# Up products of an MLP with both token parts in one 512-column matmul, and norm factors moved behind the down product

## The chip, the cores and the metric

The kernel runs on one NeuronCore of a Trainium2 chip. The metric is the device time of one execution in microseconds (us), the median of three runs.

## The reference, cut to what matters

The network has two parts. The first block has two layers (DEPTH = 2) over T = 256 tokens of width D = 1024: attention and convolution branches ("mix"), then an MLP of hidden width 4096. The second block has another attention and a product-key expert layer ("peer"). The change is in the MLP of the first block:

```python
def rmsnorm(x, g):
    y = xf * lax.rsqrt(jnp.mean(xf * xf, axis=-1, keepdims=True) + EPS)
    return (y * g.astype(jnp.float32)).astype(x.dtype)
...
        u = rmsnorm(x, norm_mlp[l])
        x = x + jnp.square(jax.nn.relu(u @ w_mlp_up[l])) @ w_mlp_down[l]
```

The norm's factor is one positive number for each token, so it can be left out of `u` and applied later: to the up product's result once, or, squared, to the down product's result.

## The kernel before, in words

**Split products.** Every fp32 operand of a large matmul is a sum of two parts, hi and lo, and each product is three matmuls: hi with hi, hi with lo, lo with hi. A `Stream` loads weights in blocks of 128x1024 or so (`raw`, by SyncE's DMA queue); ACT copies the hi part (`whi`, L92), DVE subtracts for the lo part (`wlo`, L93). There are six buffers for `whi` and `wlo`, and the splits run six blocks ahead: L92 of block j+6 writes the buffer that block j's matmuls have just read, and so it waits for the last matmul of block j that reads `whi`.

**The up stage.** The hidden width is made in 32 chunks of 128. One chunk is one weight block and eight pieces of the width D (KC = 8). `wtype` issues for each piece the three matmuls of `mm3` (L121 hi with hi, L122 hi with lo, L123 lo with hi), each 256 columns (the tokens): 24 matmuls for a chunk. The first four chunks (`split_first`) use four PSUM buffers `pf`. The other 28 go in 14 pairs: a pair shares one PSUM buffer `pw` [128, 2, 256] of the pool `psw`, which has two buffers. When both chunks of the pair are done, DVE takes relu times the norm factors (L673, `rl` from `pw` and `rows`, 512 columns), ACT squares into `hhi` (L675), DVE squares `rl` in place (L676) and subtracts for `hlo` (L677).

**The norm factors.** `factor_rows` turns the two columns of factors into a tile `rows` with a factor for each token along the free axis: two transposes on PE (L276) and a copy on ACT (L277), once a layer, behind the first four chunks.

**The down stage.** `ttype` multiplies `hhi` and `hlo` with the down weights into four accumulators (`acc`, matmuls L357 to L359) and `add` (L196) adds each 128x512 result to `x` on DVE. `norm_twice_cols` does the same for the last layer, with the next norms.

**What sets the order.** The framework's scheduler lays down each engine's instructions in one fixed order when the program is built. Each engine then works through its list in order; an instruction that waits for a semaphore holds up all that stand behind it on that engine. What one buffer costs when it is still in use is such a wait.

**In the peer part** the same products for the query and expert weights are already made with 8 matmuls of 512 columns (L926: `whi` with hi and lo of the tokens side by side) and 8 of 256 (L928: `wlo` with hi) for a block; ACT then copies one half of the PSUM buffer (L931) and DVE adds the other half (L932).

Of the kernel before, what the change touches and what calls it, by code (L numbers as in the profile page):

```python
# [18 lines left out]
P = 128  # L19
T = 256  # L20
NT = 2
D = 1024
KC = D // P
# [13 lines left out]
PK = 16  # L37
# [79 lines left out]


def mm3(nc, out, a, b, first, last):
# [73 lines left out]

def add(k, x, t, h, acc):
    s = x[:, t, h * 512:(h + 1) * 512]
    k.nc.vector.tensor_tensor(out=s, in0=acc[t][h], in1=s, op=ALU.add)  # L196

# [45 lines left out]

def scaled_cols(k, stream, x, norm, first=False):

    nc = k.nc
    u = [k.acts.tile([P, KC, T], F32R, name=n, tag=n) for n in ("uhi", "ulo")]
    gB = k.work.tile([P, D], F32, name="gB", tag="gB", bufs=2)  # L250
    nc.sync.dma_start(out=gB, in_=norm.to_broadcast([P, D]))
    xg = [k.work.tile([P, D], F32, name="xg", tag="xn", bufs=2) for _ in range(NT)]
    done = []

    def each(acc, t, h):
        c = slice(h * 512, (h + 1) * 512)
        if acc is not None:
            add(k, x, t, h, acc)
# [20 lines left out]

def norm_twice_cols(k, stream, pool, x, acc, fB, gB, sB, hi, lo):  # L280

# [33 lines left out]
    with k.tc.manual_schedule(engines={nc.vector.engine}):  # L315
        add(k, x, 0, 0, acc)
        times(0, 0, nc.vector)
        scaled(0, 0, nc.gpsimd)
        add(k, x, 0, 1, acc)
# [4 lines left out]
        add(k, x, 1, 0, acc)  # L324
        times(1, 0, nc.gpsimd)
        scaled(1, 0, nc.gpsimd)
        hi_part(0, 0)
        add(k, x, 1, 1, acc)
        hi_part(0, 1)
# [79 lines left out]


def split_first(k, stream, u, n):


    pss = [k.psa.tile([P, T], F32, name="pf", tag="acc") for _ in range(n)]
    ws = [stream.next(i) for i in range(n)]
    for part in (range(0, 4), range(4, KC)):
        for ps, w in zip(pss, ws):
            end = wtype(k, w, 0, u, KC, ps, part)
    return pss, end
# [109 lines left out]
def layer(k, l, stream, x, u, rs):  # L529
# [3 lines left out]
    with k.tc.tile_pool(name="att", bufs=1, reuse_waits="tile") as att:  # L533
# [107 lines left out]
        ttype(k, stream, (mhi, mlo), 8, 1, 512, 2, tail=TAIL_MIX, swap=True, each=each)  # L641
    rows = k.work.tile([P, T], F32, name="rows", tag="rows", bufs=1)
    rs = factors()
    with k.tc.tile_pool(name="mlp", bufs=1, reuse_waits="tile") as mlp:
# [15 lines left out]
        first, end = split_first(k, stream, u, FIRST)  # L660
        with k.tc.issue_after(end):
            factor_rows(k, rs, rows)
        for j in range(0, HID // P, 2):
            r = mlp.tile([P, 2, T], F32, name="rl", tag="rl", bufs=3)
            if first:
                for i in range(2):
                    nc.vector.scalar_tensor_tensor(out=r[:, i, :], in0=first.pop(0), scalar=0.0, in1=rows,
                                                   op0=ALU.max, op1=ALU.mult)
            else:
                ps = k.psw.tile([P, 2, T], F32, name="pw", tag="w")  # L670
                for i in range(2):
# [12 lines left out]
        if l < DEPTH - 1:  # L684
            u, each, factors = scaled_cols(k, stream, x, k.a["norm_mix"][l + 1:l + 2, :], True)
# [5 lines left out]
        u = [k.acts.tile([P, KC, T], F32R, name=n, tag=n) for n in ("uhi", "ulo")]  # L691
        norm_twice_cols(k, stream, mlp, x, acc, *last[0], *u)
        return u, None

# [210 lines left out]

def peer(k, x, pool, hp, stream, u, both):

# [3 lines left out]
    with ExitStack() as es:  # L911
# [8 lines left out]
        def up(e2, done, gl):  # L920

            w = stream.next()
            ps = k.psa.tile([P, 2, T], F32, name="pw", tag="acc")
            for c in range(KC):
                o = slice(c * P, (c + 1) * P)
                nc.tensor.matmul(ps.rearrange("p i t -> p (i t)"), w[0][:, o], both[:, c].rearrange("p i t -> p (i t)"),  # L926
                                 start=c == 0, stop=False)
                end = nc.tensor.matmul(ps[:, 0, :], w[1][:, o], u[0][:, c, :], start=False, stop=c == KC - 1).ins  # L928

            def total(out, part):  # L930
                nc.scalar.activation(out, ps[:, 1, part], AF.Copy)  # L931
                nc.vector.tensor_tensor(out=out, in0=ps[:, 0, part], in1=out, op=ALU.add)  # L932
                nc.scalar.activation(out, out, AF.Gelu_apprx_tanh)
# [23 lines left out]
        with k.tc.tile_pool(name="tk", bufs=1, reuse_waits="tile") as tk:  # L957
# [26 lines left out]
            def select():  # L984
                for h in range(H):
# [16 lines left out]
                    if h % 2 == 0:  # L1002
                        vs = tk.tile([P, 2, NT, PK], F32, name="vs", tag="vs", bufs=2)
                    vi = tk.tile([P, NT, PK], U32, name="vi", tag="vi", bufs=2)
                    for t in range(NT):
# [216 lines left out]
def body(tc, a):  # L1222
# [3 lines left out]
    with ExitStack() as es:  # L1226
# [21 lines left out]
        with ExitStack() as ph:  # L1248
# [22 lines left out]
            hp = es.enter_context(tc.tile_pool(name="hp", bufs=1, side="right", reuse_waits="tile"))  # L1271
            both = hp.tile([P, KC, 2, T], F32R, name="h2", tag="h2")
            u = [both[:, :, 0, :], both[:, :, 1, :]]
# [4 lines left out]
        peer(k, x, pool, hp, stream, u, both)  # L1278

# [117 lines left out]
```

## Time and profile before

| | us |
|---|---|
| median of 3 runs | 1693.84 |
| the runs | 1691.16 to 1696.8 |
| the profiled execution, its time | 1690.12 |
| its span, first to last instruction | 1688.3 |

In the rows below, times are us from the start of the span, unless they are marked ns. An engine's "busy" is the time in which one of its instructions ran. "[0.87 <-DVE wlo L93]" behind an instruction says that its engine sat idle for 0.87 us before it, until line 93 on DVE had written `wlo`. A matmul's end is modelled and successive matmuls overlap; what one costs is the distance from its start to the next start.

### The profile page before, as it was taken

Reading aid. Unit: us, or ns where it says so; the run is one execution under the profiler, and the core shown is the slowest. Engines: PE = TensorE matmul, PEld = TensorE weight load, DVE = VectorE, ACT = ScalarE, POOL = GpSimd, SP = SyncE. Lnnn points to the kernel's source line nnn. Section 1 sums busy time; section 2 is a strip of 40 time slices with the busy share of each in tenths; the row PEclk is TensorE's granted clock in tenths of the full one; section 3 lists DMA queues with packets and bytes.
Section 4 is the critical chain, followed back from the end, with each engine's and each line's share of the span. In section 5 each row is a group of like instructions: output and inputs, shape, how many; then the busy total and the mean of one; then the engine's idle time right before and its main releaser. Section 6 shows DMA issues by size and latency. Waiting matters only on the chain.

```text
span 1688.3 us, 27147 instructions
## 1 busy us (share of the span) xinstructions
PE 1653.2 (98%) x10082; PEld 1468.1 (87%) x10082; DVE 1296.1 (77%) x2257; ACT 906.3 (54%) x1575; POOL 299.1 (18%) x227
## 2 busy tenths in 40 slices
PE   8999999999999999999999999999999999999997
PEld 7899899888999999878878889888888787888886
DVE  6867788767867778866768999998999876555555
ACT  6554545336554544344555665667777544444443
POOL 1000000000000000025400586777810000000000
PEclk9999999999999999999999999999999999999999
DMA  8566578976456667967226678777755887666664
GB/s 315 180 198 218 192 241 293 366 258 200 139 152 185 214 199 257 360 203 241 88 80 195 179 178 204 176 177 168 159 153 164 263 281 224 190 191 193 190 193 129
DMA packets 115715, 345.58 MB, mean 205 GB/s; under 512 B 29856, under 2 KB 31104, under 8 KB 114688
## 3 DMA queue, kind: packets, MB, share of 16 engines
q1 hardware_dynamic: 95104, 336.23, 61.7%
q0 software_dynamic: 20480, 7.63, 4.2%
q8 instruction: 79, 1.29, 0.3%
q14 instruction: 52, 0.43, 0.1%
HBM read 342.66 MB, written 11.64 MB: 210 GB/s over the span
## 4 chain that ended last, share of the span: by engine, by line
PE 79%; DVE 11%; DMA 4%; ACT 2%; issue 2%; POOL 1%; SPq 0%; POOLq 0%; DVEq 0%; ACTq 0%
PE acc L358 12%; PE acc L357 12%; PE acc L359 12%; PE pw L123 9%; PE pw L121 9%; PE pw L122 9%; PE pw L926 8%; PE pw L928 4%; DVE wlo L93 4%; DMA gt<-gscr 3%; PE pst L1095 1%; PE po L477 1%; ACT whi L92 1%; DVE big L932 1%; DVE big L1097 1%
## 5 line engine op out<-in xcount | busy, mean ns | idle before, releaser
L93 DVE TENSOR_TENSOR wlo<-raw,whi 128x1024 fp32r<-128x1024 f32 (+1 forms) x549 | 669.0, 1221 | 211.9 <-ACT whi L92 209.2
L92 ACT ACTIVATE whi<-raw 128x1024 fp32r<-128x1024 f32 (+1 forms) x549 | 572.9, 1047 | 481.9 <-PE acc L359 210.2
L926 PE MATMUL pw<-h,whi 128*128 128x512 f32 x1024 | 362.9, 398 | 0.0
L928 PE MATMUL pw<-h,wlo 128*128 128x256 f32 x1024 | 285.6, 279 | 0.0
L121 PE MATMUL pw<-uhi,whi 128*128 128x256 f32 x1000 | 285.1, 285 | 0.0
L122 PE MATMUL pw<-ulo,whi 128*128 128x256 f32 x1000 | 284.2, 284 | 0.0
L123 PE MATMUL pw<-uhi,wlo 128*128 128x256 f32 x1000 | 284.2, 284 | 0.0
L946 POOL DMA_INDIRECT gscr<-gate,place x128 | 221.5, 1730 | 130.2 <-DVE first L1049 67.2
L926 PEld LDWEIGHTS pw<-h,whi 128*128 128x128 f32 x1024 | 192.3, 188 | 43.0
L358 PE MATMUL acc<-wlo,ah 128*128 128x512 f32 x512 | 201.9, 394 | 0.9 <-DVE wlo L93 0.9
L357 PE MATMUL acc<-whi,ah 128*128 128x512 f32 x512 | 201.0, 393 | 1.7 <-DVE big L932 1.7
L359 PE MATMUL acc<-whi,al 128*128 128x512 f32 x512 | 198.7, 388 | 0.0
L122 PEld LDWEIGHTS pw<-ulo,whi 128*128 128x128 f32 x1000 | 192.4, 192 | 1.3 <-issue 1.3
L121 PEld LDWEIGHTS pw<-uhi,whi 128*128 128x128 f32 x1000 | 192.5, 192 | 0.9 <-issue 0.7
L928 PEld LDWEIGHTS pw<-h,wlo 128*128 128x128 f32 x1024 | 192.9, 188 | 0.2 <-DVE wlo L93 0.2
L123 PEld LDWEIGHTS pw<-uhi,wlo 128*128 128x128 f32 x1000 | 192.4, 192 | 0.7 <-issue 0.7
L357 PEld LDWEIGHTS acc<-whi,ah 128*128 128x128 f32 x512 | 96.1, 188 | 25.1 <-issue 2.8
L359 PEld LDWEIGHTS acc<-whi,al 128*128 128x128 f32 x512 | 96.1, 188 | 21.8 <-DVE al L128 0.4
L358 PEld LDWEIGHTS acc<-wlo,ah 128*128 128x128 f32 x512 | 96.3, 188 | 20.7 <-DVE wlo L93 1.7
L357 PE MATMUL acc<-whi,hhi 128*128 128x512 f32 x256 | 99.9, 390 | 0.0
L358 PE MATMUL acc<-wlo,hhi 128*128 128x512 f32 x256 | 99.8, 390 | 0.0
L359 PE MATMUL acc<-whi,hlo 128*128 128x512 f32 x256 | 99.6, 389 | 0.0
(265 smaller groups left out, 2524.3 us busy)
## 6 DMA issues: line engine op xcount, KB each, us to landing
raw<-in_w_layers_dram SPq DMA_DIRECT2D x240, 512.0 KB
raw<-in_u_dram SPq DMA_DIRECT2D x128, 512.0 KB
raw<-in_v_dram SPq DMA_DIRECT2D x128, 512.0 KB
aw<-in_w_ada_dram SPq DMA_DIRECT2D x48, 512.0 KB
gscr<-in_zeros_dram SPq DMA_DIRECT2D x16, 512.0 KB
raw<-in_w_query_dram SPq DMA_DIRECT2D x16, 512.0 KB
gt<-gscr SPq DMA_DIRECT2D x32, 256.0 KB
raw<-in_w_qkb_dram SPq DMA_DIRECT2D x8, 512.0 KB
```

The costliest lines, as they stand in the source:

```text
L92: self.nc.scalar.activation(hi[:, :w], r[:, :w], AF.Copy)
L93: self.last_split = self.nc.vector.tensor_sub(lo[:, :w], r[:, :w], hi[:, :w]).ins
L121: nc.tensor.matmul(out, a[0], b[0], start=first, stop=False)
L122: nc.tensor.matmul(out, a[0], b[1], start=False, stop=False)
L123: return nc.tensor.matmul(out, a[1], b[0], start=False, stop=last).ins
L357: nc.tensor.matmul(acc, a[0], w[0][:, o:o + cols], start=first, stop=False)
L358: nc.tensor.matmul(acc, a[0], w[1][:, o:o + cols], start=False, stop=False)
L359: return nc.tensor.matmul(acc, a[1], w[0][:, o:o + cols], start=False, stop=last).ins
L477: nc.tensor.matmul(po[:, h, :], pT[:, i, :], v[:, c, vcol(h):vcol(h) + DH], start=(c == 0), stop=(c == nchunk - 1))
L926: nc.tensor.matmul(ps.rearrange("p i t -> p (i t)"), w[0][:, o], both[:, c].rearrange("p i t -> p (i t)"), start=c == 0, stop=False)
L928: end = nc.tensor.matmul(ps[:, 0, :], w[1][:, o], u[0][:, c, :], start=False, stop=c == KC - 1).ins
L946: ins = nc.gpsimd.indirect_dma_start(out=k.gscr, out_offset=bass.IndirectOffsetOnAxis(ap=place[:, h, j:j + 1], axis=0), in_=gate[:, h, j:j ...
```

## The change

The two parts of `u` become one tile with hi and lo side by side (`parts`), and the MLP's up product uses the form of the peer part: `wtype_both` issues 8 matmuls of 512 columns and 8 of 256 for a chunk. Its result takes a whole `psw` buffer for one chunk, since the products with `u` hi and `u` lo lie in separate halves, and `halves` brings them together: a copy on ACT (L450) and an add on DVE (L451), 128x256 each, for each of the 64 chunks. Then DVE makes relu(r) times r (L712), ACT copies the hi part (L713) and DVE subtracts (L714), once for a pair. `factor_rows` goes from the MLP; its factors are squared (`squared`, two DVE instructions of 128x1 a layer) and `add` multiplies the down result with them while it adds (four instructions in each layer, 128x512 as before, with one more operand). `vi`, a small tile of the peer part, has one buffer where it had two.

```diff
+def wtype_both(k, w, u, nk, out, part=None):
+    for c in part or range(nk):
+        o = slice(c * P, (c + 1) * P)
+        k.nc.tensor.matmul(out.rearrange("p i t -> p (i t)"), w[0][:, o], u.both[:, c].rearrange("p i t -> p (i t)"),
+                           start=c == 0, stop=False)
+        end = k.nc.tensor.matmul(out[:, 0, :], w[1][:, o], u[0][:, c, :], start=False, stop=c == nk - 1).ins
+    return end
+
+def halves(k, out, ps):
+    k.nc.scalar.activation(out, ps[:, 1, :], AF.Copy)
+    return k.nc.vector.tensor_tensor(out=out, in0=ps[:, 0, :], in1=out, op=ALU.add).ins
...
-def add(k, x, t, h, acc):
+def add(k, x, t, h, acc, factors=None):
     s = x[:, t, h * 512:(h + 1) * 512]
-    k.nc.vector.tensor_tensor(out=s, in0=acc[t][h], in1=s, op=ALU.add)
+    if factors is None:
+        k.nc.vector.tensor_tensor(out=s, in0=acc[t][h], in1=s, op=ALU.add)
+    else:
+        k.nc.vector.scalar_tensor_tensor(out=s, in0=acc[t][h], scalar=factors[t], in1=s, op0=ALU.mult, op1=ALU.add)
...
-        with k.tc.issue_after(end):
-            factor_rows(k, rs, rows)
         for j in range(0, HID // P, 2):
             r = mlp.tile([P, 2, T], F32, name="rl", tag="rl", bufs=3)
-            if first:
-                for i in range(2):
-                    nc.vector.scalar_tensor_tensor(out=r[:, i, :], in0=first.pop(0), scalar=0.0, in1=rows,
-                                                   op0=ALU.max, op1=ALU.mult)
-            else:
-                ps = k.psw.tile([P, 2, T], F32, name="pw", tag="w")
-                for i in range(2):
-                    wtype(k, stream.next(), 0, u, KC, ps[:, i, :])
-                nc.vector.scalar_tensor_tensor(out=r, in0=ps, scalar=0.0,
-                                               in1=rows[:, None, :].to_broadcast([P, 2, T]), op0=ALU.max, op1=ALU.mult)
-            nc.scalar.activation(hhi[:, j:j + 2, :], r, AF.Square)
-            nc.vector.tensor_tensor(out=r, in0=r, in1=r, op=ALU.mult)
+            for i in range(2):
+                if first:
+                    ps = first.pop(0)
+                else:
+                    ps = k.psw.tile([P, 2, T], F32, name="pw", tag="w")
+                    wtype_both(k, stream.next(), u, KC, ps)
+                halves(k, r[:, i, :], ps)
+            nc.vector.scalar_tensor_tensor(out=r, in0=r, scalar=0.0, in1=r, op0=ALU.max, op1=ALU.mult)
+            nc.scalar.activation(hhi[:, j:j + 2, :], r, AF.Copy)
             up = nc.vector.tensor_sub(hlo[:, j:j + 2, :], r, hhi[:, j:j + 2, :]).ins
```

**DVE in the middle of layer 0's up stage, before:** two periods of a pair.

```order
L673 SCALAR_TENSOR_TENSOR rl<-pw,rows 128x512
L93 TENSOR_TENSOR wlo<-raw,whi 128x1024
L676 TENSOR_TENSOR rl<-rl 128x512
L677 TENSOR_TENSOR hlo<-rl,hhi 128x512
L93 TENSOR_TENSOR wlo<-raw,whi 128x1024
L673 SCALAR_TENSOR_TENSOR rl<-pw,rows 128x512
L93 TENSOR_TENSOR wlo<-raw,whi 128x1024
L676 TENSOR_TENSOR rl<-rl 128x512
```

**The same place of the change,** two periods (`pw` is the PSUM buffer of one chunk; the chunk whose L451 stands behind L714 is the even one of its pair, the next L451 is the odd one's):

```order
L93 TENSOR_TENSOR wlo<-raw,whi 128x1024
L714 TENSOR_TENSOR hlo<-rl,hhi 128x512
L451 TENSOR_TENSOR rl<-pw,rl 128x256
L93 TENSOR_TENSOR wlo<-raw,whi 128x1024
L451 TENSOR_TENSOR rl<-pw,rl 128x256
L712 SCALAR_TENSOR_TENSOR rl<-rl 128x512
L93 TENSOR_TENSOR wlo<-raw,whi 128x1024
L714 TENSOR_TENSOR hlo<-rl,hhi 128x512
L451 TENSOR_TENSOR rl<-pw,rl 128x256
L93 TENSOR_TENSOR wlo<-raw,whi 128x1024
L451 TENSOR_TENSOR rl<-pw,rl 128x256
```

Where one L673 for a pair stood between two weight splits, each chunk now has its own add. The even chunk's add stands third, behind the split (L93) of the block six further on and behind the last step (L714) of the pair before.

**ACT at that place, before and in the change:**

```order
L675 ACTIVATE hhi<-rl 128x512
L92 ACTIVATE whi<-raw 128x1024 x2
L675 ACTIVATE hhi<-rl 128x512
L92 ACTIVATE whi<-raw 128x1024 x2
L675 ACTIVATE hhi<-rl 128x512
L92 ACTIVATE whi<-raw 128x1024 x2
```

```order
L713 ACTIVATE hhi<-rl 128x512
L450 ACTIVATE rl<-pw 128x256
L92 ACTIVATE whi<-raw 128x1024
L450 ACTIVATE rl<-pw 128x256
L92 ACTIVATE whi<-raw 128x1024
L713 ACTIVATE hhi<-rl 128x512
```

The two copies L450 stand behind the weight splits L92, the even one behind L713 of the pair before as well. The first `L442` of a chunk carries a wait for the L451 of the chunk two before it, whose PSUM buffer it takes.

**PE near the end of layer 0's up stage in the change** (`acc` with `whi` and `hhi` is the down product):

```order
L442 MATMUL pw<-u,whi 128x512
L444 MATMUL pw<-u,wlo 128x256
L442 MATMUL pw<-u,whi 128x512
L444 MATMUL pw<-u,wlo 128x256
L383 MATMUL acc<-whi,hhi 128x512
L384 MATMUL acc<-wlo,hhi 128x512
L385 MATMUL acc<-whi,hlo 128x512
L383 MATMUL acc<-whi,hhi 128x512
L442 MATMUL pw<-u,whi 128x512
```

Four matmuls of the down product now stand in front of the first chunk of the last pair, and three in front of that of the pair before; so it is in both layers. In the kernel before no down product stands between the up products. Elsewhere in the program the order of PE, DVE, ACT and POOL is the same but for buffer numbers; in SyncE's queue some loads of the up stage changed places.

## Rows read from the trace of the kernel before

**Rows 1.** The page: busy time and share of the span; then the chain's engines.

```profile
PE 1653.2 (98%) x10082; PEld 1468.1 (87%) x10082; DVE 1296.1 (77%) x2257; ACT 906.3 (54%) x1575; POOL 299.1 (18%) x227
...
PE 79%; DVE 11%; DMA 4%; ACT 2%; issue 2%; POOL 1%; SPq 0%; POOLq 0%; DVEq 0%; ACTq 0%
```

**Rows 2.** Stretches: length, busy and instructions of each engine, clock, DMA; layer 0's up stage.

```profile
211.70:292.40 80.70, 80.70 (x675) 80.70 (x674) 68.87 (x85) 40.14 (x46) 1.02 (x2) 1.00 0.79 265
```

**Rows 3.** Groups by shape, same stage: count | busy, mean ns | idle before, releaser.

```profile
L121 PE MATMUL pw<-uhi,whi 128*128 128x256 f32 x224 | 63.5, 283 | 0.0
...
L93 DVE TENSOR_TENSOR wlo<-raw,whi 128x1024 fp32r<-128x1024 f32 x29 | 35.4, 1222 | 6.0 <-ACT whi L92 6.0
L92 ACT ACTIVATE whi<-raw 128x1024 fp32r<-128x1024 f32 x28 | 29.7, 1061 | 35.5 <-PE pw L122 21.6 <-issue 11.7 <-ACT hhi L675 1.2
```

**Rows 4.** Timeline, one pair's end in layer 0 (start, duration, engine, line).

```profile
240.58 0.28 PE L121 MATMUL pw<-uhi,whi 128*128 128x256 f32 x1
...
240.71 1.06 ACT L92 ACTIVATE whi<-raw 128x1024 fp32r<-128x1024 f32 x1 [1.82 <-PE pw L122]
240.78 0.69 DVE L673 SCALAR_TENSOR_TENSOR rl<-pw,rows 128x512 f32<-128x512 f32 x1 [0.63 <-PE pw L123]
...
241.81 1.22 DVE L93 TENSOR_TENSOR wlo<-raw,whi 128x1024 fp32r<-128x1024 f32 x1 [0.33 <-ACT whi L92]
...
242.95 0.68 DVE L676 TENSOR_TENSOR rl<-rl 128x512 f32<-128x512 f32 x1
...
243.67 0.69 DVE L677 TENSOR_TENSOR hlo<-rl,hhi 128x512 fp32r<-128x512 f32 x1
```

**Rows 5.** Timeline, peer part with its 512- and 256-column matmuls.

```profile
899.80 0.40 PE L926 MATMUL pw<-h,whi 128*128 128x512 f32 x1
...
902.40 0.41 DVE L932 TENSOR_TENSOR big<-pw,big 128x256 f32<-128x256 f32 x1
...
903.17 0.37 ACT L931 ACTIVATE big<-pw 128x256 f32<-128x256 f32 x1
...
905.00 0.39 PE L926 MATMUL pw<-h,whi 128*128 128x512 f32 x1
```

**Rows 6.** Timeline, PE between first chunks and the rest, layer 0.

```profile
211.46 0.28 PE L123 MATMUL pf<-uhi,wlo 128*128 128x256 f32 x1
...
211.58 0.38 PE L276 MATMUL pr<-ident,pw 128*128 128x128 f32 x2
...
211.72 0.36 PE L121 MATMUL pw<-uhi,whi 128*128 128x256 f32 x1
...
211.92 0.28 PE L122 MATMUL pw<-ulo,whi 128*128 128x256 f32 x1
```

**Rows 7.** Timeline, a PE wait for DVE in the value stage.

```profile
1394.88 1.22 DVE L93 TENSOR_TENSOR wlo<-raw,whi 128x1024 fp32r<-128x1024 f32 x1
...
1396.15 0.51 PE L358 MATMUL acc<-wlo,ah 128*128 128x512 f32 x1 [0.87 <-DVE wlo L93]
...
1396.49 0.40 PE L359 MATMUL acc<-whi,al 128*128 128x512 f32 x1
...
1396.73 0.40 PE L357 MATMUL acc<-whi,ah 128*128 128x512 f32 x1
```

**Rows 8.** Timeline, DVE, two instructions of 512 columns in a row.

```profile
197.25 0.69 DVE L260 TENSOR_TENSOR xg<-x,gB 128x512 f32<-128x512 f32 x1
...
197.86 0.68 DVE L182 TENSOR_TENSOR ulo<-pst,uhi 128x512 fp32r<-128x512 f32 x1
```

**Rows 9.** Stretches, columns as in rows 2: the first four chunks, layer 0.

```profile
199.20:211.70 12.50, 12.50 (x105) 12.22 (x104) 9.33 (x14) 9.71 (x17) 1.68 (x3) 1.00 0.44 137
```

**Rows 10.** Stretches, columns as in rows 2: start of the second block, peer part.

```profile
754.50:758.00 3.50, 3.50 (x15) 3.50 (x15) 2.94 (x7) 3.03 (x5) 2.13 (x3) 0.51 0.43 125
882.00:1320.00 438.00, 436.71 (x2735) 390.63 (x2734) 405.84 (x1014) 298.40 (x695) 221.46 (x128) 1.00 0.69 176
```

**Rows 11.** Timeline, PE at the second block's start.

```profile
751.45 0.63 PE L175 MATMUL pst<-ident,xg 128*128 128x128 f32 x4 [2.05 <-DVE xg L308]
```

More of the change, by code (lines that the diff above doesn't have):

```diff
@@ L116, with parts @@
     pass
+class Parts(list):
+    pass
+def parts(pool, chunks, name):
+    both = pool.tile([P, chunks, 2, T], F32R, name=name, tag=name)
+    u = Parts((both[:, :, 0, :], both[:, :, 1, :]))
+    u.both = both
+    return u
 def mm3(nc, out, a, b, first, last):
@@ L191, in to_cols, with squared @@
     return done
-def add(k, x, t, h, acc):
+def add(k, x, t, h, acc, factors=None):
     s = x[:, t, h * 512:(h + 1) * 512]
-    k.nc.vector.tensor_tensor(out=s, in0=acc[t][h], in1=s, op=ALU.add)
+    if factors is None:
+        k.nc.vector.tensor_tensor(out=s, in0=acc[t][h], in1=s, op=ALU.add)
+    else:
+        k.nc.vector.scalar_tensor_tensor(out=s, in0=acc[t][h], scalar=factors[t], in1=s, op0=ALU.mult, op1=ALU.add)
+def squared(k, rs):
+    out = []
+    for r in rs:
+        s = k.small.tile([P, 1], F32, name="rr", tag="rr")
+        k.nc.vector.tensor_tensor(out=s, in0=r, in1=r, op=ALU.mult)
+        out.append(s)
+    return out
 def norm_cols(k, x, acc, gB, sB, hi, lo):
@@ L241, in norm_cols, with scaled_cols @@
     return ps[1, 1][1], done
-def scaled_cols(k, stream, x, norm, first=False):
+def scaled_cols(k, stream, x, norm, first=False, times=None):
     nc = k.nc
-    u = [k.acts.tile([P, KC, T], F32R, name=n, tag=n) for n in ("uhi", "ulo")]
+    u = parts(k.acts, KC, "u")
     gB = k.work.tile([P, D], F32, name="gB", tag="gB", bufs=2)
@@ L257, in each @@
         if acc is not None:
-            add(k, x, t, h, acc)
+            add(k, x, t, h, acc, times)
         with k.tc.issue_after(done[1][1]) if acc is None and t else ExitStack():
@@ L277, in factor_rows, with norm_twice_cols @@
     k.nc.scalar.activation(rows, ps, AF.Copy)
-def norm_twice_cols(k, stream, pool, x, acc, fB, gB, sB, hi, lo):
+def norm_twice_cols(k, stream, pool, x, acc, factors, fB, gB, sB, hi, lo):
     nc = k.nc
@@ L315, in norm_twice_cols @@
     with k.tc.manual_schedule(engines={nc.vector.engine}):
-        add(k, x, 0, 0, acc)
+        add(k, x, 0, 0, acc, factors)
         times(0, 0, nc.vector)
         scaled(0, 0, nc.gpsimd)
-        add(k, x, 0, 1, acc)
+        add(k, x, 0, 1, acc, factors)
         times(0, 1, nc.vector)
@@ L323, in norm_twice_cols @@
         r12[0] = power(k, "r12", z)
-        add(k, x, 1, 0, acc)
+        add(k, x, 1, 0, acc, factors)
         times(1, 0, nc.gpsimd)
@@ L327, in norm_twice_cols @@
         hi_part(0, 0)
-        add(k, x, 1, 1, acc)
+        add(k, x, 1, 1, acc, factors)
         hi_part(0, 1)
@@ L408, in wtype @@
     return end
+def wtype_both(k, w, u, nk, out, part=None):
[8 more added lines that the diff above has]
+    return k.nc.vector.tensor_tensor(out=out, in0=ps[:, 0, :], in1=out, op=ALU.add).ins
 def split_first(k, stream, u, n):
-    pss = [k.psa.tile([P, T], F32, name="pf", tag="acc") for _ in range(n)]
+    pss = [k.psa.tile([P, 2, T], F32, name="pf", tag="acc") for _ in range(n)]
     ws = [stream.next(i) for i in range(n)]
@@ L417, in split_first @@
         for ps, w in zip(pss, ws):
-            end = wtype(k, w, 0, u, KC, ps, part)
+            end = wtype_both(k, w, u, KC, ps, part)
     return pss, end
@@ L641, in layer @@
         ttype(k, stream, (mhi, mlo), 8, 1, 512, 2, tail=TAIL_MIX, swap=True, each=each)
-    rows = k.work.tile([P, T], F32, name="rows", tag="rows", bufs=1)
-    rs = factors()
+    rr = squared(k, factors())
     with k.tc.tile_pool(name="mlp", bufs=1, reuse_waits="tile") as mlp:
@@ L684, in layer @@
         if l < DEPTH - 1:
-            u, each, factors = scaled_cols(k, stream, x, k.a["norm_mix"][l + 1:l + 2, :], True)
+            u, each, factors = scaled_cols(k, stream, x, k.a["norm_mix"][l + 1:l + 2, :], True, rr)
         else:
@@ L690, in layer @@
             return u, factors()
-        u = [k.acts.tile([P, KC, T], F32R, name=n, tag=n) for n in ("uhi", "ulo")]
-        norm_twice_cols(k, stream, mlp, x, acc, *last[0], *u)
+        u = parts(k.acts, KC, "u")
+        norm_twice_cols(k, stream, mlp, x, acc, rr, *last[0], *u)
         return u, None
@@ L903, in peer_stream, with peer @@
     return Stream(k.tc, pool, blocks, D, 3, 3, 3, 2)
-def peer(k, x, pool, hp, stream, u, both):
+def peer(k, x, pool, hp, stream, u):
     nc = k.nc
@@ L923, in up @@
             ps = k.psa.tile([P, 2, T], F32, name="pw", tag="acc")
[L924 to L928, printed above, removed]
+            end = wtype_both(k, w, u, KC, ps)
             def total(out, part):
-                nc.scalar.activation(out, ps[:, 1, part], AF.Copy)
-                nc.vector.tensor_tensor(out=out, in0=ps[:, 0, part], in1=out, op=ALU.add)
+                halves(k, out, ps[:, :, part])
                 nc.scalar.activation(out, out, AF.Gelu_apprx_tanh)
@@ L1003, in select @@
                         vs = tk.tile([P, 2, NT, PK], F32, name="vs", tag="vs", bufs=2)
-                    vi = tk.tile([P, NT, PK], U32, name="vi", tag="vi", bufs=2)
+                    vi = tk.tile([P, NT, PK], U32, name="vi", tag="vi", bufs=1)
                     for t in range(NT):
@@ L1271, in body @@
             hp = es.enter_context(tc.tile_pool(name="hp", bufs=1, side="right", reuse_waits="tile"))
-            both = hp.tile([P, KC, 2, T], F32R, name="h2", tag="h2")
-            u = [both[:, :, 0, :], both[:, :, 1, :]]
+            u = parts(hp, KC, "h2")
             pool = es.enter_context(tc.tile_pool(name="peer", bufs=1, side="right", reuse_waits="tile"))
@@ L1277, in body @@
             stream.after = norm_cols(k, x, *norm, *u)
-        peer(k, x, pool, hp, stream, u, both)
+        peer(k, x, pool, hp, stream, u)
 def _pack_t(w, c):
```

## The prediction

> **What bounds the kernel now.** I read the page first: PE is busy for 98% of the span, and the chain of work that ended last lies on PE for 79% of it and on DVE for 11% [rows 1]. So the question for each edit is what it does to PE's queue. Then the stretch of the up stage by engine: layer 0's 28 chunks behind the first four take 80.70 us, PE is busy in all of it at the full clock, DVE for 68.87 us and ACT for 40.14 us [rows 2]. 672 matmuls in 80.70 us are 0.120 us from start to start, and no idle stands ahead of the matmuls [rows 3]. PE alone sets this stage: a chunk is 24 x 0.120 = 2.88 us. DVE is off the path, yet used for 85%.
>
> Next the timeline at the end of a pair. The next chunk starts at 240.58. ACT begins the split of a new weight block at 240.71, when the last read of the old `whi` is over, and DVE begins L673, which empties the pair's PSUM buffer, at 240.78; then come the `wlo` half of the split, L676 and L677 [rows 4]. The buffer is free at about 241.5, and is wanted again when the other pair is done, 5.76 us after 240.58. This cover, some 4.8 us, is what the change uses up: a PSUM buffer now holds one chunk, not two, so it is wanted again after one chunk.
>
> **The change part by part.**
>
> *Matmuls.* A chunk becomes 8 matmuls of 512 and 8 of 256 columns. The peer part issues just this: from 899.80 to 905.00 are 15 pairs, so 0.347 us for one [rows 5] and 2.77 us for a chunk, against 2.88 us. That saves 0.106 us a chunk, for 64 chunks **-6.8 us**. Columns are as many as before; what goes is the fixed part of 512 matmuls, 13 ns each by these rows (6.8/512). In the Trainium skill, "TensorE: Matmul & The Clock Gate", section "Wait — 56ns, not 53.3ns?", a matmul at the full clock costs its columns and about 2.5 ns; by that page the saving would be an estimated 1.3 us, and the whole sum below 5.5 us higher. The rows are of this very form of product and give five times the page's figure; I go by them and leave the other no chance.
>
> *Norm factors.* `factor_rows` stood between an L123 at 211.46 and an L121 at 211.72, followed at 0.20 us by the next: 0.46 us for what would be 0.24 [rows 6]. Gone in two layers: **-0.4 us**. The two new DVE instructions on 128x1 a layer fall where DVE is busy for 9.33 of 12.50 us [rows 9]; nothing. Without that cover they would cost at most four times a 128x256 add, 1.6 us. The down result's add keeps its size, and the three-operand form was no slower: L673, from PSUM, took 0.69 us, like L677 [rows 4]; nothing.
>
> *DVE's and ACT's work.* For a pair DVE loses two 512-column instructions (0.69 + 0.68) and gets two adds of 0.41 and one of 0.69 us: +0.1 us. ACT gets two copies of 0.37 us [rows 4, 5]. In 5.5 us neither is full: DVE's 68.87 becomes about 70 of 78 us, ACT's 40.14 about 51. No engine becomes the bound by its sum.
>
> *The order, where I expect the loss.* The rows of the order show what stands ahead of the even chunk's add on DVE: the weight split six blocks on (L93), then L714 of the pair before. That split can't start before the even chunk's own matmuls are over, since its `whi` buffer is the one that they read. Take the start of the odd chunk's matmuls as zero:
> - ACT starts L92 at 0.13 (240.71 - 240.58), takes 1.06, and L93 follows 0.04 later, at 1.23 (241.81) [rows 4].
> - L93 to the next start on DVE: 1.14 (241.81 to 242.95) [rows 4]. L714 starts at 2.37. It waits for L713 on ACT, which stands behind L92 and ends near 1.8, so not for that.
> - L714 to the next: 0.61 (197.25 to 197.86) [rows 8]. L451 starts at 2.98, and its copy L450, third on ACT, ends near 2.1. It takes 0.41 [rows 5]: free at 3.39.
> - DVE to PE: 0.05 (L93 ends at 1396.10, the matmul starts at 1396.15) [rows 7]. PE may go on at **3.44**, but is done with the odd chunk at 2.77.
>
> So PE is without work for 0.67 us at the start of every even chunk. The first matmul after a wait also took 0.34 us to the next, where 0.24 is usual (1396.15, 1396.49, 1396.73) [rows 7]: +0.10, together 0.77 us. The odd chunk's buffer is not late: its split ends at about 5.1, its add at 5.6, and PE wants it at 3.44 + 2.87 = 6.3. A pair then takes 2.77 + 0.67 + 0.10 + 2.77 = 6.31 us, against 5.76. Waiting doesn't cure itself, because the next split again waits for PE.
>
> How often: in the order of layer 0 the rows L93, L714, L451 stand so for chunks 6 to 18, 22, 24 and later, in layer 1 for 4, 6, 10 to 24 and later (even ones). The last two of each layer free buffers for chunks 28 and 30, where three and four matmuls of the down product stand in front; at 0.24 us each (1396.49 to 1396.73 [rows 7]) they cover 0.7 and 1.0 us, which is enough for a 0.67. That leaves 9 and 10 places: 19 x 0.77 = **+14.6 us**. The bounds: nothing, if DVE somehow comes earlier; and 28 x 0.77 = 21.6 if all 14 pairs of both layers wait. I take the 19 that the order shows.
>
> Sum: 14.6 - 6.8 - 0.4 = **+7.4 us**, worked from an execution of 1690.12 us, of which 1688.3 is the span; it lies 3.7 us below the median of the runs, and I put the change on the median: 1693.84 + 7.4 = 1701.2 us. The change of `vi` and the swapped loads I cost at nothing: DMA moved 265 GB/s here with its engines busy for 79%, and no matmul waited for a weight [rows 2, 3]; a stage that is stretched by waits asks for less.
>
> **Rivals.**
> - *The gain comes through* (the other side). If the even chunk's add ended before 2.77 on that clock, no wait would arise and the change gives -6.8 - 0.4: 1686.6 us. For it: the sums of DVE and ACT leave room. Against: 0.67 us would have to go out of a chain of six terms, each with its row; it is decided if L92 needn't wait for the even chunk. Chance 0.11.
> - *Only some of the waits.* 11.7 of L92's 35.5 us idle is put down to no event [rows 3]. If a third of the splits start without regard to their chunk, 13 waits stay: 10.0 - 7.2 = +2.8, 1696.6 us; if half of the wait is there everywhere, +0.1. Chance 0.24, most of it inside 0.3%.
> - *More waits.* All 14 pairs of both layers: 21.6 - 7.2 = +14.4, 1708.2 us, if ACT's copies come late as well. Chance 0.06.
> - *The clock falls.* PE ran near half clock from 754.50 to 758.00 (0.51) [rows 10], shortly after it had waited 2.05 us [rows 11]; in the peer part it stayed at 1.00 for 438 us with about 1.3 us of idle in all [rows 10]. The up stage will idle 0.67 us in every 6.3. One such half-clock stretch costs half of 3.5 us; one in each layer +3.5 on top: 1704.7 us. In the Trainium skill the same page, section "A second HAM failure mode: psum-queue depth-cycling", tells of a kernel whose clock went to and fro because PE paused briefly between groups of matmuls; the rows here show no fall after waits under 1 us, the 0.87 us of rows 7 for one. Chance 0.05.
>
> **How the numbers follow.** The forecast, waits at about 19 places, has 0.54, its own range 1698 to 1705. The five chances add up to 1. For the range I leave out most of the rival that gains and the far end of the last two: 1692 to 1708. About 0.3% (5.1 us) is what a measurement of this kernel can tell from no change: slower lies above 1698.9, faster below 1688.8. Slower: the forecast with nearly all of its 0.54, both of the last rivals less a little, together 0.62; within: the partial waits and the forecast's low edge, 0.27; faster: 0.11.
>
> **What would show it.** In the changed trace: 2.77 us for a chunk without wait; idle of 0.6 to 0.8 us ahead of L442 put down to DVE L451, every second chunk, some 19 times, about 13 us in all; L93, L714, L451 close together on DVE before each; layer 0's stage from the first `pw` to the last about 86 us (80.7 - 3.0 + 6.9, and 1.6 of down matmuls), layer 1's 87; the gap of rows 6 gone; the peer part and all else as before. I am wrong if PE doesn't wait at those places, if L92 starts ahead of its chunk's end, if the granted clock leaves 1.00 in the stage, or if the time comes back elsewhere.

## The result, and the profile after

Median of the change: 1708.3 us (1706.49 to 1710.21, 6 runs), of the kernel before 1695.32 (1691.16 to 1702.31, 6 runs). The ratio is 1.0072, interval 1.005 to 1.0095: slower by 12 us, between 8 and 16. The forecast was +7.4. The profiled execution of before took 1690.12 us, less than any of its six runs, so the two spans differ by more, 1706.6 against 1688.3, 18.3 us. By stage of these two executions:

| | before | after | difference |
|---|---|---|---|
| MLP of layer 0, first `pf` to the last down matmul | 182.17 | 185.87 | +3.7 |
| MLP of layer 1 | 180.19 | 184.72 | +4.5 |
| start of the second block to the first peer product | 131.94 | 134.15 | +2.2 |
| peer products | 442.54 | 442.84 | +0.3 |
| value stage to the end | 364.83 | 371.87 | +7.0 |
| all else | 386.65 | 387.12 | +0.5 |

The MLP did about what was forecast. As much again came from stages that the change was not thought to touch. The page of the changed kernel, which answers to [rows 1]:

```profile
PE 1663.9 (97%) x9566; PEld 1441.2 (84%) x9566; DVE 1296.5 (76%) x2289; ACT 921.9 (54%) x1637; POOL 302.8 (18%) x227
...
PE 84%; DVE 10%; ACT 2%; issue 2%; DMA 1%; POOL 1%; SPq 0%; POOLq 0%; DVEq 0%; ACTq 0%
```

PE's share of the chain rose from 79% to 84% while its busy share fell: more of the span now hangs on PE alone, and PE has more gaps. The two up stages with their first four chunks (length; busy and instructions of PE, PEld, DVE, ACT, POOL; clock; DMA), to set against [rows 2, 9]:

```profile
199.70:298.20 98.50, 94.69 (x526) 79.82 (x525) 78.34 (x113) 57.51 (x92) 2.25 (x4) 1.00 0.69 235
573.00:672.30 99.30, 95.09 (x526) 79.96 (x525) 78.29 (x113) 57.10 (x92) 2.25 (x4) 1.00 0.60 197
```

They are 98.5 and 99.3 us long (1.6 us of it the down matmuls that now stand inside), PE is idle for 3.8 and 4.2 us of them at the full clock, and ACT works 57 us. DVE, at 78 us, isn't full. What PE waited for at L442 in the whole kernel (us in total, times, longest):

```profile
PE pw L442 <- DVE rl L451: 8.0, 19, 0.6
```

Nineteen times, as the order of the rows said. One of them in the timeline (start, duration, engine, line), the chain that the prediction wrote down from [rows 4, 5, 7, 8]:

```profile
232.63 0.39 PE L442 MATMUL pw<-u,whi 128*128 128x512 f32 x1
...
232.72 1.06 ACT L92 ACTIVATE whi<-raw 128x1024 fp32r<-128x1024 f32 x1 [2.17 <-PE pw L442]
...
233.68 0.61 ACT L713 ACTIVATE hhi<-rl 128x512 fp32r<-128x512 f32 x1
...
233.81 1.23 DVE L93 TENSOR_TENSOR wlo<-raw,whi 128x1024 fp32r<-128x1024 f32 x1 [1.22 <-ACT whi L92]
...
234.20 0.36 ACT L450 ACTIVATE rl<-pw 128x256 f32<-128x256 f32 x1
...
234.95 0.69 DVE L714 TENSOR_TENSOR hlo<-rl,hhi 128x512 fp32r<-128x512 f32 x1
...
235.29 0.28 PE L444 MATMUL pw<-u,wlo 128*128 128x256 f32 x1
...
235.55 0.42 DVE L451 TENSOR_TENSOR rl<-pw,rl 128x256 f32<-128x256 f32 x1
...
236.03 0.50 PE L442 MATMUL pw<-u,whi 128*128 128x512 f32 x1 [0.46 <-DVE rl L451]
...
236.36 0.28 PE L444 MATMUL pw<-u,wlo 128*128 128x256 f32 x1
```

The odd chunk starts at 232.63. ACT's split follows at 232.72, DVE's at 233.81 (forecast 1.23 after the start, here 1.18), L714 at 234.95 (2.37; 2.32), L451 at 235.55 (2.98; 2.92), and PE goes on at 236.03 (3.44; 3.40). The odd chunk's last matmul began at 235.29, so PE has 0.74 us where 0.12 is usual, and the next step takes 0.33 where it was 0.23. Read the idle column with care: it says 0.46, since a matmul's end is modelled; the loss is the distance of the starts. Summed in this way, waits and restarts cost 13.1 us of the two stages, 0.69 for each.

The value stage is the surprise. It has the same matmuls in the same order in both kernels. Thirty of them in the kernel before, from the first row to the second:

```profile
1440.22 0.39 PE L357 MATMUL acc<-whi,ah 128*128 128x512 f32 x1
...
1447.09 0.39 PE L357 MATMUL acc<-whi,ah 128*128 128x512 f32 x1
```

and thirty in the changed kernel:

```profile
1450.35 0.39 PE L383 MATMUL acc<-whi,ah 128*128 128x512 f32 x1
...
1457.35 0.39 PE L383 MATMUL acc<-whi,ah 128*128 128x512 f32 x1
```

6.87 us against 7.00, that is 228.9 and 233.3 ns from start to start; over 1536 matmuls 6.8 us. The clock is 1.00 in both. A smaller part is the clock itself, in stretches of the changed execution that the profiled execution of before ran at full speed:

```profile
847.60:854.50 6.90, 6.90 (x19) 4.64 (x19) 4.78 (x5) 2.69 (x8) 0.00 (x0) 0.51 0.00 0
1339.00:1343.00 4.00, 4.00 (x11) 3.14 (x11) 2.76 (x8) 0.98 (x5) 0.00 (x0) 0.57 1.08 314
```

The first is 6.8 us at 1.2 GHz and the second 3.4 us, worth at most half of that in time. In both executions PE had waited 1.4 us for DVE at the start of the value stage, at 1338.83 in the change and at 1326.89 in the kernel before; behind this wait the clock fell in the change, and in the kernel before it stayed up. Such stretches came and went in all kernels of this study (two to five in a profile, not counting the start and the end of the span), so I count them as what an execution happens to meet.

### The profile page after: what moved, and what is told of

It is laid out like the page before. It is cut to its first block, busy times and chain, and to the rows that moved or that the text cites. A ratio compares the mean times of both kernels' runs of the same rounds, so it can differ in the third digit from the quotient of the medians.

```text
span 1706.6 us, 26203 instructions
## 1 busy us (share of the span) xinstructions
PE 1663.9 (97%) x9566; PEld 1441.2 (84%) x9566; DVE 1296.5 (76%) x2289; ACT 921.9 (54%) x1637; POOL 302.8 (18%) x227
## 3 DMA queue, kind: packets, MB, share of 16 engines
q8 instruction: 75, 1.23, 0.3%
## 4 chain that ended last, share of the span: by engine, by line
PE 84%; DVE 10%; ACT 2%; issue 2%; DMA 1%; POOL 1%; SPq 0%; POOLq 0%; DVEq 0%; ACTq 0%
PE pw L442 15%; PE acc L385 13%; PE acc L383 13%; PE acc L384 13%; PE pw L444 7%; PE pw L135 5%; PE pw L134 5%; PE pw L133 5%; DVE wlo L93 3%; PE pst L1127 1%; PE po L520 1%; ACT whi L92 1%; PE pst L187 1%; DVE big L451 1%; PE sc L861 1%
## 5 line engine op out<-in xcount | busy, mean ns | idle before, releaser
L93 DVE TENSOR_TENSOR wlo<-raw,whi 128x1024 fp32r<-128x1024 f32 (+1 forms) x549 | 668.0, 1221 | 226.1 <-ACT whi L92 222.7
L92 ACT ACTIVATE whi<-raw 128x1024 fp32r<-128x1024 f32 (+1 forms) x549 | 572.7, 1047 | 474.6 <-PE acc L385 224.0
L442 PE MATMUL pw<-h,whi 128*128 128x512 f32 x1024 | 362.3, 398 | 0.0
L442 PEld LDWEIGHTS pw<-h,whi 128*128 128x128 f32 x1024 | 192.3, 188 | 42.7
L385 PE MATMUL acc<-whi,al 128*128 128x512 f32 x512 | 202.4, 396 | 0.3 <-DVE al L140 0.3
L442 PE MATMUL pw<-u,whi 128*128 128x512 f32 x448 | 161.1, 402 | 8.0 <-DVE rl L451 8.0
L133 PE MATMUL pw<-u,whi 128*128 128x256 f32 x552 | 158.0, 286 | 0.0
L134 PE MATMUL pw<-u,whi 128*128 128x256 f32 x552 | 157.4, 285 | 0.0
L135 PE MATMUL pw<-u,wlo 128*128 128x256 f32 x552 | 157.4, 285 | 0.0
L444 PE MATMUL pw<-u,wlo 128*128 128x256 f32 x448 | 125.5, 280 | 0.0
L442 PEld LDWEIGHTS pw<-u,whi 128*128 128x128 f32 x448 | 84.1, 188 | 34.4 <-DVE rl L451 12.8
L134 PEld LDWEIGHTS pw<-u,whi 128*128 128x128 f32 x552 | 106.4, 193 | 1.3 <-issue 1.3
L133 PEld LDWEIGHTS pw<-u,whi 128*128 128x128 f32 x552 | 106.4, 193 | 0.9 <-issue 0.7
L135 PEld LDWEIGHTS pw<-u,wlo 128*128 128x128 f32 x552 | 106.4, 193 | 0.7 <-issue 0.7
```

What stands on the lines that cost most here:

```text
L92: self.nc.scalar.activation(hi[:, :w], r[:, :w], AF.Copy)
L93: self.last_split = self.nc.vector.tensor_sub(lo[:, :w], r[:, :w], hi[:, :w]).ins
L385: return nc.tensor.matmul(acc, a[1], w[0][:, o:o + cols], start=False, stop=last).ins
L442: k.nc.tensor.matmul(out.rearrange("p i t -> p (i t)"), w[0][:, o], u.both[:, c].rearrange("p i t -> p (i t)"), start=c == 0, stop=False)
L444: end = k.nc.tensor.matmul(out[:, 0, :], w[1][:, o], u[0][:, c, :], start=False, stop=c == nk - 1).ins
```

## The experiments

**The MLP: is it the order, the buffers, or the throughput?**

*e3_ring4* gives the chunks four PSUM buffers. The order of DVE and ACT stays as it is in most of the up stage; a few rows change places, in the middle and near the end, and no down matmul stands inside the stage any more:

```diff
-                    ps = k.psw.tile([P, 2, T], F32, name="pw", tag="w")
+                    if j % 4:
+                        ps = k.psm.tile([P, 2, T], F32, name="pw", tag="m")
+                    else:
+                        ps = k.psw.tile([P, 2, T], F32, name="pw", tag="w")
```

> The changed kernel with every second pair of chunks in the PSUM pool psm, which stands idle in this stage: four buffers in place of two, and ACT and DVE in the same order in the up stage. Theory A (the waits come from a buffer that is wanted one chunk after its use, with L93 and L714 ahead of its add): all 19 waits go, each up stage from the first pf to the down product gets some 3.1 to 3.4 us shorter than the kernel before (32 x 0.106), and the whole is 13 to 14 us faster than the changed kernel, near 1695; what is then left above 1686 is the value stage's slower spacing and the clock. Theory B (ACT and DVE are short of throughput in the up stage): waits of the same sum come back at other chunks, time within 3 us of the changed kernel.

Its two up stages (columns as above):

```profile
200.30:289.70 89.40, 89.40 (x519) 78.69 (x518) 76.13 (x111) 57.27 (x92) 2.25 (x4) 1.00 0.75 249
568.20:657.60 89.40, 89.40 (x515) 78.07 (x514) 76.25 (x110) 57.79 (x93) 1.11 (x2) 1.00 0.66 208
```

No wait for L451 is left. 89.4 us a stage, 3.8 less than the 93.2 of the kernel before; both MLPs together 354.8 us against 362.4 before and 370.6 in the change. The kernel: 1691.78 us against 1694.37, ratio 0.999 (0.9979 to 1.0002). Theory A holds, theory B falls: DVE and ACT did the same work, in nearly the same order, in less time.

*e7_sub_behind* exchanges two rows of DVE; the subtraction of the pair before is written behind the even chunk's halves. The scheduler moved a few other rows with it, as in e3, and here too no down matmul stands inside the up stage:

```diff
-                halves(k, r[:, i, :], ps)
+                done = halves(k, r[:, i, :], ps)
+                if late is not None and i == 0:
+                    with k.tc.issue_after(done):
+                        up = nc.vector.tensor_sub(*late).ins
...
-            up = nc.vector.tensor_sub(hlo[:, j:j + 2, :], r, hhi[:, j:j + 2, :]).ins
+            late = hlo[:, j:j + 2, :], r, hhi[:, j:j + 2, :]
...
+        nc.vector.tensor_sub(*late)
```

> The changed kernel with one pair of rows exchanged on DVE: hlo's subtraction of the pair before stands behind the even chunk's add, not ahead of it; two PSUM buffers, all else the same. Theory A (the wait is the chain L92, L93, L714, L451): the chain gets 0.61 us shorter, so that each wait of about 0.6 us shrinks to some 0.0 to 0.1 (3.44 - 0.61 against 2.77), idle put down to L451 from 8.0 to about 1 us or less, and the kernel is 10 to 12 us faster than the changed one, near 1697. Theory B (two buffers are too few for the copies and adds in any order): the waits stay or move to the odd chunks, 5 us or more in sum.

```profile
PE pw L442 <- DVE rl L451: 1.0, 1, 1.0
```

All nineteen are gone. The one wait that is left is a new one, ahead of chunk 22 of layer 0, where the change had none: ACT sat idle there for 2.71 us until the load of another tile (`cB`) had landed, ahead of the copy of chunk 20. At a place like the one above:

```profile
232.31 1.22 DVE L93 TENSOR_TENSOR wlo<-raw,whi 128x1024 fp32r<-128x1024 f32 x1 [0.61 <-ACT whi L92]
...
233.45 0.42 DVE L451 TENSOR_TENSOR rl<-pw,rl 128x256 f32<-128x256 f32 x1
...
233.78 0.68 DVE L715 TENSOR_TENSOR hlo<-rl,hhi 128x512 fp32r<-128x512 f32 x1
...
233.80 0.27 PE L444 MATMUL pw<-u,wlo 128*128 128x256 f32 x1
...
233.92 0.50 PE L442 MATMUL pw<-u,whi 128*128 128x512 f32 x1
...
234.26 0.28 PE L444 MATMUL pw<-u,wlo 128*128 128x256 f32 x1
```

L451 starts 1.14 us behind L93 where it was 1.74, L715 (the subtraction) has gone behind it, and PE's next chunk starts 0.12 after its predecessor: the buffer comes just in time, with the slow first step (0.34) as the only trace of it. The kernel took 1698.2 us, ratio 1.0016 (1.0007 to 1.0025), 10 less than the change. One row of 0.6 us, moved on an engine that is busy 78 of 98 us, was the regular wait.

*e4_halves_first* queues the weight splits behind the chunk's copy and add:

```diff
-    k.nc.scalar.activation(out, ps[:, 1, :], AF.Copy)
-    return k.nc.vector.tensor_tensor(out=out, in0=ps[:, 0, :], in1=out, op=ALU.add).ins
+    copy = k.nc.scalar.activation(out, ps[:, 1, :], AF.Copy).ins
+    return copy, k.nc.vector.tensor_tensor(out=out, in0=ps[:, 0, :], in1=out, op=ALU.add).ins
...
-                halves(k, r[:, i, :], ps)
+                stream.after = halves(k, r[:, i, :], ps)
```

> The changed kernel with only the order altered: the weight splits that are issued behind a chunk are queued behind this chunk's copy and add on ACT and DVE, two PSUM buffers as in the change. Theory A (order): the even chunk's add is over some 0.9 us after its last matmul, no wait is left with two buffers, and the time is that of the four-buffer kernel, near 1695. Theory B (the buffers or the throughput are the limit, whatever the order): waits of several us in sum stay.

```profile
PE pw L442 <- DVE rl L451: 2.1, 3, 1.1
```

Three waits, one of 1.1 us; 1697.96 us, ratio 1.002 (1.0008 to 1.0033), some 6 above the four buffers. Theory A was too hopeful here: the order cures the regular wait, but with two buffers an irregular place still shows. And the product itself didn't hold its pace. A 512- and a 256-column matmul together took either 346.7 or 353.3 ns. In e3 all chunks of both up stages ran at the first; in the changed kernel two of the chunks behind the first four in layer 1 and nine in layer 0 did, and the others ran at the second, a mean of 351 ns in layer 0 and 353 in layer 1. Fourteen such pairs in the changed kernel, at the slower pace:

```profile
236.48 0.40 PE L442 MATMUL pw<-u,whi 128*128 128x512 f32 x1
...
241.43 0.40 PE L442 MATMUL pw<-u,whi 128*128 128x512 f32 x1
```

In e4 both paces stand in one stage: fourteen pairs ahead of the wait at chunk 20 of layer 0 (the first two rows), and fourteen behind it (the last two):

```profile
243.66 0.39 PE L442 MATMUL pw<-u,whi 128*128 128x512 f32 x1
...
248.52 0.39 PE L442 MATMUL pw<-u,whi 128*128 128x512 f32 x1
...
269.28 0.40 PE L442 MATMUL pw<-u,whi 128*128 128x512 f32 x1
...
274.23 0.40 PE L442 MATMUL pw<-u,whi 128*128 128x512 f32 x1
```

4.86 us against 4.95. Both groups take the same two PSUM buffers in turn, so the buffers don't set the pace. It changed at the late start of chunk 20, and from there on all the chunks of e4 ran at 353.3, in layer 1 too. What a late start leaves behind in PE isn't shown, nor why some late starts lead to the slower pace and others back to the faster one. In the change 448 pairs took 5 ns more in the mean, which cost 2.3 us of the 6.8 that the matmuls were to save and leaves some 4.5.

*e5_factors_only* is the kernel before with the factors moved behind the down product (cut; `add` as in the change, and the squares written over the factors):

```diff
-        with k.tc.issue_after(end):
-            factor_rows(k, rs, rows)
...
-                nc.vector.scalar_tensor_tensor(out=r, in0=ps, scalar=0.0,
-                                               in1=rows[:, None, :].to_broadcast([P, 2, T]), op0=ALU.max, op1=ALU.mult)
+                nc.vector.tensor_scalar(out=r, in0=ps, scalar1=0.0, scalar2=None, op0=ALU.max)
```

> The kernel before with only the norm factors moved behind the down product: three products of 256 columns and one PSUM buffer for a pair as before, DVE takes only the relu from PSUM, factor_rows is gone. The price in the prediction was -0.2 us a layer: 93.08 us from the first pf to the last pw becomes 92.8 to 92.9 in both layers, no wait of PE for L673's successor; down stages as before. If the down result's add with factors were dear, the down stage would show it, by 8 times its longer duration at most.

The up stages went from 93.08 to 92.88 and 92.87 us, first `pf` to last `pw`, the down stages stayed: -0.2 a layer, as in the sum. Its one time, 1700.75, and its value stage belong to the next question.

**The value stage: what slows the same matmuls?** The tile of the squared factors takes 4 x 32 bytes in a pool that lies ahead of nearly everything, and pushes the value stage's stationary operands `ah` and `al` from byte 158624 of a partition to 158752. (The single `vi` buffer only makes room for it; e1 keeps it.) The weights that stream past lie where they lay.

*e1_inplace* writes the squares over the factors:

```diff
-        s = k.small.tile([P, 1], F32, name="rr", tag="rr")
-        k.nc.vector.tensor_tensor(out=s, in0=r, in1=r, op=ALU.mult)
-        out.append(s)
+        k.nc.vector.tensor_tensor(out=r, in0=r, in1=r, op=ALU.mult)
+        out.append(r)
```

> The changed kernel with one thing undone: the squared factors are written over the factors instead of into a small tile of their own. That tile takes 128 bytes of each partition and moves everything behind it by as much; among others the stationary operands of the value stage (ah, al) lie at 158752 in the changed kernel and at 158624 in the kernel before, and here at 158624 again; the weights, the PSUM buffers and the order of every engine are as in the changed kernel. Theory A, the place of the operands sets the pace of the value stage's matmuls (229.0 ns from start to start before, 233.4 after, 1536 of them): the spacing goes back to 229, about 6.8 us less than the changed kernel, near 1701. Theory B, the spacing follows from something else of the change (the later phase against DMA, the vi buffer): it stays at 233.4 and the time stays at 1708. In both the 19 waits of the MLP stay.

Thirty matmuls:

```profile
1450.17 0.39 PE L382 MATMUL acc<-whi,ah 128*128 128x512 f32 x1
...
1457.04 0.39 PE L382 MATMUL acc<-whi,ah 128*128 128x512 f32 x1
```

Back to 6.87 us (228.9 ns); the 19 waits stay. 1700.33 us, ratio 1.0043 (1.0025 to 1.006): 5 us less than the change by the ratios, 8 by the medians (the kernel before had 1695.32 beside the change and 1694.37 beside e1).

*e2_shift_before* is the other direction, the kernel before with 128 bytes ahead:

```diff
+        pad = k.small.tile([P, 1], F32, name="pad", tag="pad")
+        nc.vector.memset(pad, 0.0)
...
-                    vi = tk.tile([P, NT, PK], U32, name="vi", tag="vi", bufs=2)
+                    vi = tk.tile([P, NT, PK], U32, name="vi", tag="vi", bufs=1)
```

> The kernel before with a tile of 128 bytes added in the pool of small tiles and one vi buffer (so that it fits), nothing else: ah and al then lie as in the changed kernel. Theory A (place): the value stage's matmuls go from 229.0 to 233.4 ns, about 7 us slower than the kernel before, near 1702. Theory B (something else of the change): 229.0 stays and the time is that of the kernel before, within 0.3%. The MLP has no waits in either.

```profile
1450.58 0.39 PE L357 MATMUL acc<-whi,ah 128*128 128x512 f32 x1
...
1457.58 0.39 PE L357 MATMUL acc<-whi,ah 128*128 128x512 f32 x1
```

7.00 us, 233.3 ns, and 1699.02 us, ratio 1.0033 (1.002 to 1.0045), without any of the change's work.

*e6_ring4_inplace* puts the cures together (the diffs of e3 and e1).

> The changed kernel with four PSUM buffers for the chunks (as in e3_ring4) and the squared factors written in place (as in e1_inplace), so that both costs that the runs have shown are taken away. If the two add up: up and down stages 178.4 and 176.4 us as with four buffers, the value stage's matmuls at 229 ns, in all 7.5 us less than the kernel before: about 1687 against its 1694.4, ratio 0.9955. If the clock's falls or the waits of the second block eat the gain, 1690 to 1692 and no difference that shows.

1686.4 us, ratio 0.9954 (0.9938 to 0.997): the two add up. It is also the base of the next three.

*e10_operands_moved*, *e12_place256* and *e13_place64* move only the tiles behind `iota` in the value stage's own pool, by 128, 256 and 64 bytes (`P + 32`, `P + 64` and `P + 16`; the first is shown). Each ran once, in 1691.09, 1685.14 and 1682.55 us:

```diff
-            iota = gs.tile([P, P], F32, name="iota")
+            iota = gs.tile([P, P + 32], F32, name="iota")[:, :P]
```

> e6_ring4_inplace with 128 unused bytes behind iota in the value stage's own pool: only the tiles of that pool behind iota (the stationary operands ah and al, the fetched gates gt) move, to where the changed kernel has them; the large tile big and all of the first block stay where the kernel before has them. If the place of ah and al sets the spacing: 233.3 ns, the value stage 4 to 7 us longer than in e6_ring4_inplace. If it is big's place, or that of another tile: 229.

> e6_ring4_inplace with 256 unused bytes behind iota: ah and al at 158880, which is 256 past the place of the kernel before. If the pace depends on the place modulo 256 bytes, or on the distance between the tiles modulo 256: 229 ns. If any move from 158624 leads to the slow pace: 233.

> e6_ring4_inplace with 64 unused bytes behind iota: ah and al at 158688, half way between the two places known so far. A third place: 229 or 233 would say on which side of it the pace changes; 226.7, the pace of the MLP's down stage, would be a place that saves another 3.5 us (1536 x 2.3 ns).

Thirty matmuls 128 bytes on, and 64 bytes on:

```profile
1440.11 0.40 PE L382 MATMUL acc<-whi,ah 128*128 128x512 f32 x1
...
1447.11 0.40 PE L382 MATMUL acc<-whi,ah 128*128 128x512 f32 x1
```

```profile
1440.41 0.39 PE L382 MATMUL acc<-whi,ah 128*128 128x512 f32 x1
...
1447.21 0.39 PE L382 MATMUL acc<-whi,ah 128*128 128x512 f32 x1
```

7.00 us at 128 bytes (233.3 ns), 6.80 at 64 (226.7 ns); at 256 bytes it was 6.87 again (228.9 ns). So it is the tiles of that pool, and not the large tile `big`, which didn't move, and the pace has the same value 256 bytes on. `gt` moved together with `ah` and `al`, but no matmul reads it.

*e11_factors_again* repeats e5, for one thing didn't fit:

> The kernel of e5_factors_only once more, timed. In its one execution the value stage's matmuls ran at 229 ns up to about 1410 us and at 233 behind the last wait for wlo, although ah and al lie at 158624 as in the kernel before. Theory A (the place decides, that switch was a chance event): the profile shows 229 throughout and the median is near that of the kernel before, 1694 to 1696, less 0.4. Theory B (the waits of the stage's start decide, and the place only through them): 233 again in the profile, and a median near 1700.

In e5 the place is that of the kernel before, yet the pace changed in the middle of the stage (thirty matmuls, the restart behind the last wait for `wlo`, thirty matmuls):

```profile
1340.32 0.39 PE L366 MATMUL acc<-whi,ah 128*128 128x512 f32 x1
...
1347.18 0.39 PE L366 MATMUL acc<-whi,ah 128*128 128x512 f32 x1
...
1410.38 0.40 PE L368 MATMUL acc<-whi,al 128*128 128x512 f32 x1
...
1440.68 0.40 PE L366 MATMUL acc<-whi,ah 128*128 128x512 f32 x1
...
1447.68 0.40 PE L366 MATMUL acc<-whi,ah 128*128 128x512 f32 x1
```

6.86, then 7.00. In the repetition

```profile
1450.51 0.39 PE L366 MATMUL acc<-whi,ah 128*128 128x512 f32 x1
...
1457.38 0.39 PE L366 MATMUL acc<-whi,ah 128*128 128x512 f32 x1
```

it is 6.87 in the whole stage, and the time 1693.38 us, ratio 0.9991 (0.9976 to 1.0006). So the place gives the pace in thirteen of the fourteen profiles of this study, and in the other one a restart left PE at the slower one. What makes a matmul slower in that state isn't in the records.

*e14_place64_timed* times the best place.

> The kernel of e13_place64 once more, timed: four PSUM buffers, factors in place, ah and al at 158688. By the place theory the profile shows 226.7 ns again and the median is 3 to 4 us below that of e6_ring4_inplace, 1682 to 1684, ratio to the kernel before 0.993. If the one execution was lucky, as one of the factors-only kernel was unlucky: 229 again and 1686.

1683.29 us against 1694.87, ratio 0.9934 (0.992 to 0.9948); the pace was 226.7 again. This beats the kernel before by 11.6 us and the change by 23 (by the ratios) to 25 (by the medians).

## Why the prediction came out as it did

*The waits* were right in place, number and mechanism: 19, each by the chain L92, L93, L714, L451, whose times came out within 0.06 us. Their price was 13.1 us where 14.6 stood in the sum, 0.69 for 0.77. e7 shows that the chain is the cause (0.6 us out of it, and all 19 are gone), e3 that a longer ring does the same.

*The matmuls' saving* was right as a possibility and not in the change. e3 saves 7.5 us in the two MLPs, with the factors' 0.4 in it, against a forecast of 7.2. In the changed kernel the pairs behind the first four chunks took 351 to 353 ns in the mean, not 347, which leaves about 4.5 of the 6.8. The prediction took its price from one stretch of the peer part. The same form of product ran at the slower pace elsewhere in the kernel before, for instance seven pairs in 2.48 us:

```profile
887.40 0.40 PE L926 MATMUL pw<-h,whi 128*128 128x512 f32 x1
...
889.88 0.40 PE L926 MATMUL pw<-h,whi 128*128 128x512 f32 x1
```

So a saving between 3.4 us, had all 512 pairs been slow (353.3 against 360 ns), and 6.8 us was what the rows of before allowed. The stage of e3 lost 3.8 us with 256 matmuls fewer, 14 ns for each with the factors taken off. By the Trainium skill's 2.5 ns of fixed cost for a matmul ("TensorE: Matmul & The Clock Gate", section "Wait — 56ns, not 53.3ns?") the saving would have been an estimated 1.3 us. Here the measurement decides against that.

*The factors* at -0.2 a layer: measured alone, -0.2. *DVE and ACT by their sums* don't bound the stage: right, by e3.

Together the MLP lost 8.2 us in the profiles, where the sum said 7.4. That these lie so close is partly luck: the waits cost 1.5 us less than the sum had, and the matmuls saved 2.3 us less.

The whole kernel was slower by 12 us and not by 7.4; the median, 1708.3 us, lies outside the forecast's own range (1698 to 1705) and at the far end of the wider one. *What failed* is the last sentence of the sum, "The change of `vi` and the swapped loads I cost at nothing", with "the peer part and all else as before". The new tile behind it moved the operands of a stage far from the change and cost 6.8 us there, as much as the matmuls were to save. It was a term that the sum didn't have: it compared the orders of the two programs and not the places of their tiles. No row of before gave its price, but a line in the range for it was due. The two losses make 15 us, where the ratio gives 12 with an interval of 8 to 16; the 3 us more by which the two profiled executions differ lie in the second block's start, where the clock fell once more, and in 0.8 us elsewhere.

*The rivals.* "The gain comes through" fell by the waits and holds for e6 and e14, which are the change without its two costs. "Only some of the waits" fell: all 19 came. "More waits" reached the right time for a wrong reason. "The clock falls": the granted clock was 1.00 in both up stages with 19 short stops in them, where the section of the Trainium skill that the prediction named ("A second HAM failure mode: psum-queue depth-cycling" in "TensorE: Matmul & The Clock Gate") tells of a clock that goes to and fro; here the trace doesn't agree. The falls to 1.2 GHz came in the second block, in these two executions behind waits of PE of 1.4 to 2.2 us, with and without the change; other waits of that length had no fall behind them.

## What to carry to other kernels

When a PSUM buffer holds half as much, its cover halves too: write down, for the buffer's release, what stands ahead of the releasing instruction in its engine's list, in order, and compare the end with the next use; an engine that is a fifth idle can still make PE wait every second time. A longer ring (idle PSUM of another stage) was a surer cure here than the order: e3 had no wait left, e7 and e4 one and three. When a price is taken from a row, look at several stretches of the same form; here they had two paces. And after any change in tiles, compare the places of all operands of the long matmul stages, even of those that have nothing to do with it; where a stage is long, try some places of its stationary operands.

## What the runs showed of the hardware that was not expected

The same 512-column fp32 matmuls, at the full clock and with the same streams, ran at 226.7, 228.9 or 233.3 ns from start to start, according to where their 128-column stationary operands lie: 64 bytes on, at the place of the kernel before (and 256 bytes on), and 128 bytes on. Over 1536 matmuls that is 10 us from the best place to the worst. The place gave the pace in thirteen of fourteen profiles. Once, a restart behind a wait moved PE from 228.9 to 233.3 with no change of place, and it stayed there for the rest of the stage. The pairs of a 512- and a 256-column matmul in the up stage had two paces in the same way, 346.7 and 353.3 ns, with the same buffers and a late start between them (e4). What sets the pace in PE isn't shown.
